# A bilinear form on one core: weight loads regrouped into fourteen GpSimd transfers, and y spread by VectorE transposes

## The chip, the cores and the metric

The kernel runs on one core of a Trainium2 chip. The metric is device time in microseconds (us) for one execution. The time before is the median of four runs; the profile is of one more execution.

## What is computed

```python
def setup_inputs():
    batch, dim_i, dim_j, dim_k = 32, 256, 256, 128
    ...

def reference(x, y, weight):
    return np.einsum('bi,bj,kij->bk', x, y, weight).astype(np.float32)
```

x is (batch, dim_i), y (batch, dim_j) and weight (dim_k, dim_i, dim_j), all float32. For each of 128 values of k there is a 256 x 256 matrix. The output for a batch row b and a k is x[b] times that matrix times y[b]. The weights are 33.55 MB in float32; x, y and the output are 32, 32 and 16 KB.

## The kernel before, in words

**Groups.** The 128 values of k are cut into 32 groups of four: group g holds k = g, g + 32, g + 64 and g + 96 (KK = 4 values, G = 32 groups). A group is 1 MiB in float32. Its 128 partitions are (ip, kk): 32 blocks of i by the four k, and in each partition lie 8 rows i (IC = 8) of 256 j, 8 KiB that are contiguous in DRAM. `w_v` (L47) is this view; in it the four k of a group are 8 MiB apart.

**Loads.** Group 0 is loaded as float32 by SyncE (L82) into `w0` and turned into bfloat16 by ScalarE (L112). All other groups are loaded by GpSimd's queue, which converts float32 to bfloat16 on the way into `w_sb` (L94 to L101): one transfer each for groups 1 to 30, and four for the last group, in pieces of 4, 2, 1 and 1 of the 8 rows (`LAST`). Each transfer has its own semaphore. After the second one GpSimd makes the identity matrix `ident` (L103, L104). GpSimd issues in this order and waits for nothing but its own memset; no buffer is reused, so no load waits for compute.

**Left operand.** VectorE builds `xblk` (L126 to L153): x is repeated four times (`x_rep`), put on the partitions by four 32-wide transposes (L132), and multiplied by a mask taken from `ident` (L142), once for each kk (L147). For each of the 8 rows ic this gives a 128 x 128 bfloat16 matrix that multiplies the four k of a group at once, with the result on 128 partitions (b, kk).

**y.** `y4` is y on the same 128 partitions (b, kk). VectorE makes a 32 x 128 `spread` matrix from the identity (L139), TensorE (PE) multiplies y by it in float32 (L157), and VectorE copies the result out of PSUM (L162).

**Units.** The groups are worked on in units of 8, 8, 6, 4, 3, 2 and 1 (`UNITS`). In a unit the groups go in pairs, one PSUM bank for each pair. For each ic in turn PE runs one matmul for each pair (128 x 512, or 128 x 256 for a single group; L166, recorded by the helper `product`), and the eight ic add up in PSUM. The first matmul of a pair waits for the semaphores of its two groups (L197); for the last group each piece is waited for at its first ic (L195). So the first matmul of a pair can run when its own groups are there, and everything after the last pair's first matmul waits for the whole unit. Then VectorE multiplies the unit's sums by `y4` (L216, PSUM to SBUF) and adds up over j (L220) into the unit's columns of `acc`; for the unit of one both are one instruction (L224). Units take PSUM banks in turn; PE waits before a unit until VectorE has read the banks it takes (L186).

**End.** SyncE stores `acc` (L233) when VectorE is done.

The order on each engine is the order of these statements; there is no scheduler that changes it. The order of loading is that of the loop at L94, and DMA transfers of one queue are worked through in the order of their issue.

Of the kernel before, what the change touches and what calls it, by code (L numbers as in the profile page):

```python
# [6 lines left out]


UNITS = (8, 8, 6, 4, 3, 2, 1)

LAST = ((0, 4), (4, 6), (6, 7), (7, 8))
BANKS = 8
# [3 lines left out]
def kernel(  # L16
# [24 lines left out]
    assert sum(UNITS) == G and UNITS[-1] == 1 and B == 32  # L41

    def sbuf(name, shape, dtype):
        return nc.alloc_sbuf_tensor(name, shape, dtype).ap()


    w_v = weight.rearrange("(kk g) (ip ic) j -> g ip kk (ic j)", kk=KK, ic=IC)  # L47

    w_sb = sbuf("w_sb", [P, G, IC * J], bf16)
    w0 = sbuf("w0", [P, IC * J], f32)  # L50
    x_sb = sbuf("x_sb", [B, I], f32)
    y_sb = sbuf("y_sb", [B, J], f32)
    ident = sbuf("ident", [P, P], f32)
    mask = sbuf("mask", [P, KK], f32)
    spread = sbuf("spread", [B, B, KK], f32)
# [4 lines left out]
    tmp = sbuf("tmp", [P, 2, max(UNITS), J], f32)  # L60
    acc = sbuf("acc", [P, G], f32)
    ps = nc.alloc_psum_tensor("ps", [P, BANKS, 2, J], f32).ap()


    s_w = [nc.alloc_semaphore(f"w{g}") for g in range(1, G - 1)]
# [13 lines left out]


    for ins in (
        nc.sync.dma_start(out=w0, in_=w_v[0]).then_inc(s_w0, 16),  # L82
        nc.scalar.dma_start(out=x_sb, in_=x).then_inc(s_x, 16),
        nc.scalar.dma_start(out=y_sb, in_=y).then_inc(s_y, 16),
    ):
        tc.no_tile_sem_insts.add(ins.ins.name)
# [4 lines left out]
    pool, act, v, pe, sp = nc.gpsimd, nc.scalar, nc.vector, nc.tensor, nc.sync  # L91


    for g in range(1, G):  # L94
        if g < G - 1:
            pool.dma_start(out=w_sb[:, g, :], in_=w_v[g]).then_inc(s_w[g - 1], 16)  # L96
# [12 lines left out]

    for h in range(2):  # L110
        lo, hi = h * IC * J // 2, (h + 1) * IC * J // 2
        c = act.copy(out=w_sb[:, 0, lo:hi], in_=w0[:, lo:hi])  # L112
        if h == 0:
            c._wait_ge(s_w0, 16)
        c.then_inc(s_act, 1)
# [4 lines left out]
    def done(ins):  # L120
        nonlocal n_dve
        n_dve += 1
        ins.then_inc(s_dve, 1)
        return n_dve

    t = done(v.tensor_copy(  # L126
        out=x_rep,
        in_=x_sb.rearrange("b (ip ic) -> b ic ip", ic=IC).unsqueeze(3)
        .to_broadcast([B, IC, IP, KK]),
    )._wait_ge(s_x, 16))  # L130
    for q in range(Q):
# [10 lines left out]
    t = done(v.tensor_reduce(  # L142
        out=mask, in_=ident.rearrange("p (ip kk) -> p kk ip", kk=KK), axis=AX, op=add,
    ))

    for kk in range(KK):
        c = v.tensor_scalar(  # L147
            out=xblk[:, :, :, kk], in0=xt, scalar1=mask[:, kk:kk + 1],
            scalar2=None, op0=mult,
        )  # L150
# [2 lines left out]
        t_x = done(c)  # L153


    pe.wait_ge(s_y, 16)
    pe.matmul(  # L157
        out=ps[:, BANKS - 1, 0, :], lhsT=spread.rearrange("p b kk -> p (b kk)"),
        rhs=y_sb, start=True, stop=True,
    )._wait_ge(s_dve, t_spread).then_inc(s_pe, 1)  # L160
    n_pe = 1
    t_y = done(v.tensor_copy(out=y4, in_=ps[:, BANKS - 1, 0, :])._wait_ge(s_pe, n_pe))  # L162
    v.wait_ge(s_dve, t_y)

    def product(out, lhsT, rhs, first, last, load):
        return pe.add_instruction(mybir.InstMatmult(  # L166
            name=nc.get_next_instruction_name(), engine=mybir.EngineType.PE,
            ins=[pe.lower_ap(rhs), pe.lower_ap(lhsT)], outs=[pe.lower_ap(out)],
            start_tensor_calc=first, stop_tensor_calc=last,
            tile_size=(P, P), tile_position=(0, 0), ldweights=load,  # L170
        ))

    pe.wait_ge(s_dve, t_x)
    at_dve = t_x
    freed = [0] * (BANKS - 1) + [t_y]
    g0 = bank = 0
    held = None
    for u, n_g in enumerate(UNITS):

        n_b = (n_g + 1) // 2  # L180
        if bank + n_b > BANKS:
            bank = 0
        pairs = [(bank + h, g0 + 2 * h, min(2, n_g - 2 * h)) for h in range(n_b)]
        free = max(freed[bank:bank + n_b])
        if free > at_dve:
            pe.wait_ge(s_dve, free)  # L186
            at_dve = free

        up = (len(UNITS) - 1 - u) % 2 == 0
        order = range(IC) if up else range(IC - 1, -1, -1)  # L190
        for n_ic, ic in enumerate(order):
            for b, g, n in pairs:
                waits = []
                if g == G - 1:
                    waits = [s for s, (lo, _) in zip(s_last, LAST) if lo == ic]  # L195
                elif n_ic == 0:
                    waits = [s_w[h - 1] for h in range(max(g, 1), g + n)]  # L197
                if n_ic == 0 and g == 0:
                    pe.wait_ge(s_act, 2)
                for s in waits[:-1]:  # L200
                    pe.wait_ge(s, 16)
                c = product(
                    ps[:, b, :n, :], xblk[:, ic, :, :].rearrange("p b kk -> p (b kk)"),
                    w_sb[:, g:g + n, ic * J:(ic + 1) * J],
                    first=(n_ic == 0), last=(n_ic == IC - 1), load=(held != ic),
                )
                held = ic
                if waits:
                    c._wait_ge(waits[-1], 16)
                if n_ic == IC - 1 and g + n == g0 + n_g:  # L210
                    c.then_inc(s_pe, 1)
        n_pe += 1
        prod = tmp[:, u % 2, :n_g, :]
        sums = ps[:, bank:bank + n_b, :, :].rearrange("p a h j -> p (a h) j")[:, :n_g, :]
        if n_g > 1:
            t = done(v.tensor_tensor(  # L216
                out=prod, in0=sums, in1=y4.unsqueeze(1).to_broadcast([P, n_g, J]), op=mult,
            )._wait_ge(s_pe, n_pe))
            freed[bank:bank + n_b] = [t] * n_b
            done(v.tensor_reduce(  # L220
                out=acc[:, g0:g0 + n_g], in_=prod, axis=AX, op=add,
            )._wait_ge(s_dve, t))
        else:
            done(v.tensor_tensor_reduce(  # L224
                out=prod[:, 0, :], in0=sums[:, 0, :], in1=y4, scale=1.0, scalar=0.0,
                op0=mult, op1=add, accum_out=acc[:, g0:g0 + 1],
            )._wait_ge(s_pe, n_pe))
        bank += n_b
        g0 += n_g


    out_v = out.rearrange("b (kk g) -> b kk g", kk=KK)
# [37 lines left out]
```

## Time and profile before

| | before |
|---|---|
| median of four runs | 86.81 us (86.5 to 87.32) |
| profiled execution, its own time | 86.88 us |
| its span, first to last instruction | 85.4 us |
| PE busy | 40.5 us (47%), 138 matmuls |
| VectorE (DVE) busy | 23.3 us (27%) |
| GpSimd (POOL) busy | 19.9 us (23%) |
| GpSimd queue: packets, bytes written | 4896, 16.26 MB |
| HBM read | 33.62 MB, 394 GB/s over the span |
| mean granted PE clock | 0.86 |

The profile's own execution took 86.88 us, of which 85.4 are the span from the first to the last instruction; 1.5 us lie around it. The page divides the span into 40 slices and gives each engine's busy share in tenths; "PEclk" is the clock that PE was granted and "GB/s" what DMA moved, counted at the writing side. The chain of work is followed back from the last instruction to what released it. "DVE" is VectorE, "POOL" GpSimd, "SP" SyncE, "PEld" PE's weight loads. Line numbers (L166) are those of the kernel before.

### The profile page before, as it was taken

The page shows a single profiled execution, that of the slowest core. Times are in us where ns is not written, and L with a number is a line of the kernel's source. Part 1 is how long each engine was busy: PE and PEld are TensorE (multiplying, and loading weights), DVE is VectorE, ACT ScalarE, POOL GpSimd, SP SyncE. Part 2 cuts the span into 40 slices and gives each one's busy share as a digit, 9 for nine tenths or more (in the row PEclk, how much of TensorE's full clock was granted, in tenths as well). Part 3 has the DMA queues.
Part 4 walks back from the last instruction along what each step waited for, and adds up shares of the span by engine and source line. Part 5 has one row for each costly group of instructions (what it writes and reads, how often), then busy time and mean ns, then how long its engine had stood idle before and what let it go on. Part 6 is the DMA issues. An engine that isn't in the chain of part 4 may idle for free.

```text
span 85.4 us, 323 instructions
## 1 busy us (share of the span) xinstructions
PE 40.5 (47%) x138; PEld 6.2 (7%) x52; DVE 23.3 (27%) x26; ACT 3.3 (4%) x3; POOL 19.9 (23%) x40
## 2 busy tenths in 40 slices
PE   0052002020199961020099992009997392099980
PEld 0020000000000100000010100001110020022240
DVE  0893000000000049700000009910003937300672
ACT  0635000000000000000000000000000000000000
POOL 0699999999600000000000000000000000000000
PEclk9999999999999999955556999975569999755699
DMA  0999999999999999999999999999999999999930
GB/s 15 365 282 213 213 213 200 211 213 211 211 215 215 215 213 213 211 211 207 213 213 215 215 215 211 215 215 213 213 215 215 215 213 213 213 211 208 198 51 8
DMA packets 5280, 17.39 MB, mean 204 GB/s; under 512 B 736, under 2 KB 1184, under 8 KB 5152
## 3 DMA queue, kind: packets, MB, share of 16 engines
q0 software_dynamic: 4896, 16.26, 95.9%
q1 hardware_dynamic: 288, 1.07, 3.3%
q10 hardware_dynamic: 96, 0.07, 0.3%
HBM read 33.62 MB, written 0.02 MB: 394 GB/s over the span
## 4 chain that ended last, share of the span: by engine, by line
DMA 50%; PE 22%; POOL 14%; another core or an unknown queue 6%; DVE 2%; issue 1%; POOLq 0%
DMA w_sb<-in_weight_dram 50%; PE ps L166 22%; POOL w_sb L96 13%; DVE tmp L216 1%; DVE acc L220 1%; DVE tmp L224 0%; POOL ident L104 0%; POOL ident L103 0%; POOLq L89 0%; DVE acc L224 0%
## 5 line engine op out<-in xcount | busy, mean ns | idle before, releaser
L166 PE MATMUL ps<-w_sb,xblk 128*128 128x512 bf16 (+1 forms) x136 | 39.3, 450 | 37.1 <-DMA w_sb<-in_weight_dram 37.0
L216 DVE TENSOR_TENSOR tmp<-ps,y 128x2048 f32<-128x2048 f32 (+4 forms) x6 | 9.2, 1536 | 57.8 <-PE ps L166 57.8
L96 POOL DMA_DIRECT2D w_sb<-in_weight_dram x30 | 17.1, 773 | 2.4 <-POOLq L89 2.4
L166 PEld LDWEIGHTS ps<-w_sb,xblk 128*128 128x128 bf16 x50 | 5.7, 113 | 71.2 <-issue 68.4
L220 DVE TENSOR_REDUCE acc<-tmp 128x8 f32<-128x2048 f32 (+4 forms) x6 | 9.2, 1530 | 0.2
L157 PE MATMUL ps<-y_sb,spread 32*128 32x256 f32 x2 | 1.2, 710 | 5.3 <-DVE spread L139 5.3
L99 POOL DMA_DIRECT2D w_sb<-in_weight_dram x4 | 2.6, 1057 | 0.0
L112 ACT CAST w_sb<-w 128x1024 bf16<-128x1024 f32 x2 | 2.0, 1043 | 2.0 <-DMA w<-in_weight_dram 2.0
L132 DVE STREAM_TRANSPOSE xt<-x_rep 32x256 f32<-32x256 f32 x4 | 1.7, 435 | 0.1
L147 DVE TENSOR_SCALAR xblk<-xt,mask 128x256 bf16<-128x256 f32 x4 | 1.4, 499 | 0.0
L112 ACT ACT_TABLE_LOAD x1 | 1.3, 1283 | 2.4 <-PEq L89 2.4
L126 DVE COPY x_rep<-x_sb 32x1024 f32<-32x1024 f32 x1 | 0.7, 681 | 2.4 <-PEq L89 2.4
L157 PEld LDWEIGHTS ps<-y_sb,spread 32*128 32x128 f32 x2 | 0.5, 308 | 5.3 <-DVE spread L139 5.3
L162 DVE COPY y<-ps 128x256 f32<-128x256 f32 x1 | 0.4, 436 | 0.0
L224 DVE CUSTOM_DVE_ANT_0 tmp<-ps,y 128x256 f32<-128x256 f32 x1 | 0.4, 414 | 0.0
L142 DVE TENSOR_REDUCE mask<-ident 128x4 f32<-128x128 f32 x1 | 0.4, 357 | 0.0
L104 POOL TENSOR_SCALAR_AFFINE_SELECT ident<-ident 128x128 f32<-128x128 f32 x1 | 0.3, 287 | 0.1
L103 POOL MEMSET ident<- 128x128 f32 x1 | 0.2, 248 | 0.0
L139 DVE COPY spread<-ident 32x128 f32<-32x128 f32 x1 | 0.2, 215 | 0.0
L254 POOL MEMSET const-float32-0.0<- 128x1 f32 x1 | 0.1, 99 | 0.2 <-issue 0.2
L254 POOL MEMSET const-bfloat16-1.0<- 128x1 bf16 x1 | 0.1, 102 | 0.0
L254 POOL MEMSET const-uint8-127<- 128x1 uint8 x1 | 0.1, 102 | 0.0
(2 smaller groups left out, 0.2 us busy)
## 6 DMA issues: line engine op xcount, KB each, us to landing
w_sb<-in_weight_dram POOLq DMA_DIRECT2D x30, 512.0 KB, 32.1
w<-in_weight_dram SPq DMA_DIRECT2D x1, 1024.0 KB, 4.9
w_sb<-in_weight_dram POOLq DMA_DIRECT2D x1, 256.0 KB, 61.0
w_sb<-in_weight_dram POOLq DMA_DIRECT2D x1, 128.0 KB, 61.1
w_sb<-in_weight_dram POOLq DMA_DIRECT2D x2, 64.0 KB, 60.9
x_sb<-in_x_dram ACTq DMA_DIRECT2D x1, 32.0 KB, 1.6
y_sb<-in_y_dram ACTq DMA_DIRECT2D x1, 32.0 KB, 3.6
out_dram<-acc SPq DMA_DIRECT2D x1, 16.0 KB, 1.4
```

The costliest lines, as they stand in the source:

```text
L96: pool.dma_start(out=w_sb[:, g, :], in_=w_v[g]).then_inc(s_w[g - 1], 16)
L99: pool.dma_start(out=w_sb[:, g, lo * J:hi * J], in_=w_v[g][:, :, lo * J:hi * J],).then_inc(s, 16)
L112: c = act.copy(out=w_sb[:, 0, lo:hi], in_=w0[:, lo:hi])
L126: t = done(v.tensor_copy(out=x_rep, in_=x_sb.rearrange("b (ip ic) -> b ic ip", ic=IC).unsqueeze(3) .to_broadcast([B, IC, IP, KK]),)._wait_ ...
L132: c = v.transpose(out=xt[q * 32:(q + 1) * 32, :, :], in_=x_rep[:, :, q * IP // Q:(q + 1) * IP // Q, :],)
L142: t = done(v.tensor_reduce(out=mask, in_=ident.rearrange("p (ip kk) -> p kk ip", kk=KK), axis=AX, op=add,))
L147: c = v.tensor_scalar(out=xblk[:, :, :, kk], in0=xt, scalar1=mask[:, kk:kk + 1], scalar2=None, op0=mult,)
L157: pe.matmul(out=ps[:, BANKS - 1, 0, :], lhsT=spread.rearrange("p b kk -> p (b kk)"), rhs=y_sb, start=True, stop=True,)._wait_ge(s_dve, t_s ...
L162: t_y = done(v.tensor_copy(out=y4, in_=ps[:, BANKS - 1, 0, :])._wait_ge(s_pe, n_pe))
L166: return pe.add_instruction(mybir.InstMatmult(name=nc.get_next_instruction_name(), engine=mybir.EngineType.PE, ins=[pe.lower_ap(rhs), pe.l ...
L216: t = done(v.tensor_tensor(out=prod, in0=sums, in1=y4.unsqueeze(1).to_broadcast([P, n_g, J]), op=mult,)._wait_ge(s_pe, n_pe))
L220: done(v.tensor_reduce(out=acc[:, g0:g0 + n_g], in_=prod, axis=AX, op=add,)._wait_ge(s_dve, t))
```

## The change

The groups stay the same sets of four k, but loads, units and the places in `w_sb` are rearranged.

- `LOADS` lists ten GpSimd transfers of 1, 2, 4, 8, 4, 2, 4, 2, 1 and 2 groups; after them come the four pieces of the last group, which is now group 23. With group 0, which SyncE still loads, this covers all 32 groups. A transfer has one semaphore, whatever its size.
- The groups of one transfer are equally spaced (every 4th, 8th, 16th), so that the values of k in it are equally spaced too: a transfer of n groups reads, for each ip, 4n rows at one step (1 MiB for eight groups, 2 MiB for four, 4 MiB for two, 8 MiB for one). In each partition it writes n stretches of 4 KiB, at places in `w_sb` that are equally spaced as well.
- `UNITS` still has 8, 8, 6, 4, 3, 2 and 1 groups, named by number. `place_of` gives the place of a group in `w_sb`, so that a unit's groups lie side by side. The first matmul of a pair waits for the transfers that its groups are in, if no earlier matmul has waited for them: unit 0 waits for the first three transfers, unit 1 for that of eight, the unit of six for those of four and two, the unit of four for one of four, the unit of three for those of two and one, the unit of two for one of two, the last for the four pieces.
- VectorE's reduce writes columns of `acc` that are equally spaced; where the groups of a unit are not, there are two reduces: 4 + 2 for the unit of six, 2 + 1 for the unit of three.
- GpSimd makes `ident` after its second transfer, as before, which now is the one of groups 8 and 24.
- `y4` is made without PE: VectorE transposes y in blocks of 32 (`yt`), repeats it four times along kk (`y_rep`), and transposes the result onto the partitions in four instructions. `spread`, the two-pass float32 matmul and the copy from PSUM go.

PE's number of product matmuls and their shapes and order do not change.

```diff
-UNITS = (8, 8, 6, 4, 3, 2, 1)
+UNITS = (
+    tuple(range(0, 32, 4)),
+    tuple(range(1, 32, 4)),
+    (2, 10, 18, 26, 6, 22),
+    (3, 11, 19, 27),
+    (14, 30, 7),
+    (15, 31),
+    (23,),
+)
+LOADS = (
+    (16,), (8, 24), (4, 12, 20, 28), tuple(range(1, 32, 4)), (2, 10, 18, 26),
+    (6, 22), (3, 11, 19, 27), (14, 30), (7,), (15, 31),
+)
...
-    w_v = weight.rearrange("(kk g) (ip ic) j -> g ip kk (ic j)", kk=KK, ic=IC)
+    def rows_of(groups):
+        step = G // len(groups)
+        assert all(g == groups[0] + n * step for n, g in enumerate(groups))
+        v = weight.rearrange("(u s) (ip ic) j -> s ip u (ic j)", s=step, ic=IC)
+        return v[groups[0]]
+
+    def w_of(groups):
+        at = [place_of[g] for g in groups]
+        step = at[1] - at[0] if len(at) > 1 else 1
+        assert all(a == at[0] + n * step for n, a in enumerate(at))
+        return w_sb[:, at[0]:at[-1] + 1:step, :]
...
-    for g in range(1, G):
-        if g < G - 1:
-            pool.dma_start(out=w_sb[:, g, :], in_=w_v[g]).then_inc(s_w[g - 1], 16)
-        else:
-            for s, (lo, hi) in zip(s_last, LAST):
-                pool.dma_start(
-                    out=w_sb[:, g, lo * J:hi * J], in_=w_v[g][:, :, lo * J:hi * J],
-                ).then_inc(s, 16)
-        if g == 2:
+    for n, (load, s) in enumerate(zip(LOADS, s_w)):
+        pool.dma_start(out=w_of(load), in_=rows_of(load)).then_inc(s, 16)
+        if n == 1:
             pool.memset(ident, 0.0).then_inc(s_pool, 1)
...
+    for s, (lo, hi) in zip(s_last, LAST):
+        pool.dma_start(
+            out=w_sb[:, G - 1, lo * J:hi * J],
+            in_=rows_of(UNITS[-1])[:, :, lo * J:hi * J],
+        ).then_inc(s, 16)
...
-    t_spread = done(v.tensor_copy(
-        out=spread, in_=ident[:B, :B].unsqueeze(2).to_broadcast([B, B, KK]),
-    )._wait_ge(s_pool, 2))
...
-    pe.matmul(
-        out=ps[:, BANKS - 1, 0, :], lhsT=spread.rearrange("p b kk -> p (b kk)"),
-        rhs=y_sb, start=True, stop=True,
-    )._wait_ge(s_dve, t_spread).then_inc(s_pe, 1)
-    n_pe = 1
-    t_y = done(v.tensor_copy(out=y4, in_=ps[:, BANKS - 1, 0, :])._wait_ge(s_pe, n_pe))
-    v.wait_ge(s_dve, t_y)
+    t = done(v.transpose(
+        out=yt, in_=y_sb.rearrange("b (jb j) -> b jb j", j=32),
+    )._wait_ge(s_y, 16))
+    t = done(v.tensor_copy(
+        out=y_rep, in_=yt.unsqueeze(3).to_broadcast([B, J // 32, B, KK]),
+    )._wait_ge(s_dve, t))
+    BQ = B // Q
+    for q in range(Q):
+        c = v.transpose(
+            out=y4[q * 32:(q + 1) * 32, :].rearrange("p (jb j) -> p jb j", j=32),
+            in_=y_rep[:, :, q * BQ:(q + 1) * BQ, :],
+        )
...
+                need = [sem_of[g] for g in places[at:at + n] if g in sem_of]
+                need = [s for n_s, s in enumerate(need)
+                        if s.num not in landed and s not in need[:n_s]]
+                if u == len(UNITS) - 1:
+                    need = [s for s, (lo, _) in zip(s_last, LAST) if lo == ic]
+                landed |= {s.num for s in need}
...
-            done(v.tensor_reduce(
-                out=acc[:, g0:g0 + n_g], in_=prod, axis=AX, op=add,
-            )._wait_ge(s_dve, t))
+            lo = 0
+            while lo < n_g:
+                hi = lo + 1
+                while hi < n_g and unit[hi] - unit[hi - 1] == unit[lo + 1] - unit[lo]:
+                    hi += 1
+                step = unit[lo + 1] - unit[lo] if hi - lo > 1 else 1
+                c = v.tensor_reduce(
+                    out=acc[:, unit[lo]:unit[hi - 1] + 1:step], in_=prod[:, lo:hi, :],
+                    axis=AX, op=add,
+                )
...
```

More of the change, by code (lines that the diff above doesn't have):

```diff
@@ L40 @@
     assert KK * B == P and IP * KK == P and IC * IP == I and G * KK == K
-    assert sum(UNITS) == G and UNITS[-1] == 1 and B == 32
+    places = [g for unit in UNITS for g in unit]
+    place_of = {g: i for i, g in enumerate(places)}
+    assert sorted(places) == list(range(G)) and len(UNITS[-1]) == 1 and B == 32
     def sbuf(name, shape, dtype):
         return nc.alloc_sbuf_tensor(name, shape, dtype).ap()
-    w_v = weight.rearrange("(kk g) (ip ic) j -> g ip kk (ic j)", kk=KK, ic=IC)
+    def rows_of(groups):
[8 more added lines that the diff above has]
+        return w_sb[:, at[0]:at[-1] + 1:step, :]
     w_sb = sbuf("w_sb", [P, G, IC * J], bf16)
@@ L54 @@
     mask = sbuf("mask", [P, KK], f32)
-    spread = sbuf("spread", [B, B, KK], f32)
+    yt = sbuf("yt", [B, J // 32, B], f32)
+    y_rep = sbuf("y_rep", [B, J // 32, B, KK], f32)
     x_rep = sbuf("x_rep", [B, IC, IP, KK], f32)
@@ L59 @@
     y4 = sbuf("y4", [P, J], f32)
-    tmp = sbuf("tmp", [P, 2, max(UNITS), J], f32)
+    tmp = sbuf("tmp", [P, 2, max(map(len, UNITS)), J], f32)
     acc = sbuf("acc", [P, G], f32)
     ps = nc.alloc_psum_tensor("ps", [P, BANKS, 2, J], f32).ap()
-    s_w = [nc.alloc_semaphore(f"w{g}") for g in range(1, G - 1)]
+    s_w = [nc.alloc_semaphore(f"w{load[0]}") for load in LOADS]
+    sem_of = {g: s for s, load in zip(s_w, LOADS) for g in load}
     s_last = [nc.alloc_semaphore(f"wl{lo}") for lo, _ in LAST]
@@ L81 @@
     for ins in (
-        nc.sync.dma_start(out=w0, in_=w_v[0]).then_inc(s_w0, 16),
+        nc.sync.dma_start(out=w0, in_=rows_of((0,))).then_inc(s_w0, 16),
         nc.scalar.dma_start(out=x_sb, in_=x).then_inc(s_x, 16),
@@ L107 @@
             )._wait_ge(s_pool, 1).then_inc(s_pool, 1)
+    for s, (lo, hi) in zip(s_last, LAST):
[3 more added lines that the diff above has]
+        ).then_inc(s, 16)
     for h in range(2):
         lo, hi = h * IC * J // 2, (h + 1) * IC * J // 2
-        c = act.copy(out=w_sb[:, 0, lo:hi], in_=w0[:, lo:hi])
+        c = act.copy(out=w_sb[:, place_of[0], lo:hi], in_=w0[:, lo:hi])
         if h == 0:
@@ L138 @@
         done(c)
-    t_spread = done(v.tensor_copy(
-        out=spread, in_=ident[:B, :B].unsqueeze(2).to_broadcast([B, B, KK]),
-    )._wait_ge(s_pool, 2))
     t = done(v.tensor_reduce(
         out=mask, in_=ident.rearrange("p (ip kk) -> p kk ip", kk=KK), axis=AX, op=add,
-    ))
+    )._wait_ge(s_pool, 2))
     for kk in range(KK):
@@ L153 @@
         t_x = done(c)
-    pe.wait_ge(s_y, 16)
-    pe.matmul(
-        out=ps[:, BANKS - 1, 0, :], lhsT=spread.rearrange("p b kk -> p (b kk)"),
-        rhs=y_sb, start=True, stop=True,
-    )._wait_ge(s_dve, t_spread).then_inc(s_pe, 1)
-    n_pe = 1
-    t_y = done(v.tensor_copy(out=y4, in_=ps[:, BANKS - 1, 0, :])._wait_ge(s_pe, n_pe))
-    v.wait_ge(s_dve, t_y)
+    t = done(v.transpose(
[10 more added lines that the diff above has]
+        )
+        if q == 0:
+            c._wait_ge(s_dve, t)
+        t = done(c)
+    v.wait_ge(s_dve, t)
     def product(out, lhsT, rhs, first, last, load):
@@ L171, in product @@
         ))
+    pe.wait_ge(s_act, 2)
     pe.wait_ge(s_dve, t_x)
     at_dve = t_x
-    freed = [0] * (BANKS - 1) + [t_y]
-    g0 = bank = 0
+    n_pe = 0
+    freed = [0] * BANKS
+    landed = set()
+    p0 = bank = 0
     held = None
-    for u, n_g in enumerate(UNITS):
+    for u, unit in enumerate(UNITS):
+        n_g = len(unit)
         n_b = (n_g + 1) // 2
@@ L182 @@
             bank = 0
-        pairs = [(bank + h, g0 + 2 * h, min(2, n_g - 2 * h)) for h in range(n_b)]
         free = max(freed[bank:bank + n_b])
@@ L191 @@
         for n_ic, ic in enumerate(order):
[L192 to L200, printed above, removed]
+            for h in range(n_b):
+                n = min(2, n_g - 2 * h)
+                at = p0 + 2 * h
+                need = [sem_of[g] for g in places[at:at + n] if g in sem_of]
[4 more added lines that the diff above has]
+                landed |= {s.num for s in need}
+                for s in need[:-1]:
                     pe.wait_ge(s, 16)
                 c = product(
-                    ps[:, b, :n, :], xblk[:, ic, :, :].rearrange("p b kk -> p (b kk)"),
-                    w_sb[:, g:g + n, ic * J:(ic + 1) * J],
+                    ps[:, bank + h, :n, :],
+                    xblk[:, ic, :, :].rearrange("p b kk -> p (b kk)"),
+                    w_sb[:, at:at + n, ic * J:(ic + 1) * J],
                     first=(n_ic == 0), last=(n_ic == IC - 1), load=(held != ic),
@@ L207 @@
                 held = ic
-                if waits:
-                    c._wait_ge(waits[-1], 16)
-                if n_ic == IC - 1 and g + n == g0 + n_g:
+                if need:
+                    c._wait_ge(need[-1], 16)
+                if n_ic == IC - 1 and h == n_b - 1:
                     c.then_inc(s_pe, 1)
@@ L219 @@
             freed[bank:bank + n_b] = [t] * n_b
-            done(v.tensor_reduce(
-                out=acc[:, g0:g0 + n_g], in_=prod, axis=AX, op=add,
-            )._wait_ge(s_dve, t))
+            lo = 0
[8 more added lines that the diff above has]
+                )
+                if lo == 0:
+                    c._wait_ge(s_dve, t)
+                done(c)
+                lo = hi
         else:
@@ L225 @@
                 out=prod[:, 0, :], in0=sums[:, 0, :], in1=y4, scale=1.0, scalar=0.0,
-                op0=mult, op1=add, accum_out=acc[:, g0:g0 + 1],
+                op0=mult, op1=add, accum_out=acc[:, unit[0]:unit[0] + 1],
             )._wait_ge(s_pe, n_pe))
         bank += n_b
-        g0 += n_g
+        p0 += n_g
     out_v = out.rearrange("b (kk g) -> b kk g", kk=KK)
```

## The prediction

> **What bounds the kernel now.** I read the page's slices first, then the queue table, then the chain of work that ended last, then VectorE's timeline at the end, and last the duration spread of the GpSimd transfers.
>
> The slices (40 of 2.13 us each) and the queue table of the page:
>
> ```profile
> span 85.4 us, 323 instructions
> ...
> PE   0052002020199961020099992009997392099980
> ...
> DVE  0893000000000049700000009910003937300672
> ...
> POOL 0699999999600000000000000000000000000000
> PEclk9999999999999999955556999975569999755699
> DMA  0999999999999999999999999999999999999930
> GB/s 15 365 282 213 213 213 200 211 213 211 211 215 215 215 213 213 211 211 207 213 213 215 215 215 211 215 215 213 213 215 215 215 213 213 213 211 208 198 51 8
> ...
> q0 software_dynamic: 4896, 16.26, 95.9%
> ```
>
> DMA is full from slice 2 to slice 38; no compute engine is. GpSimd has issued everything by slice 11 and the queue then works on for 60 us, so the rate of the 16 DMA engines sets the landings, not the issue. 213 GB/s is what is written (bf16); the reads are f32, twice that, about 426 GB/s. The 4896 packets of q0 are 34 transfers of 128 data packets plus 16 semaphore packets, one of these on each engine: 34 x 144 = 4896.
>
> The chain that ended last, in order of time:
>
> ```profile
> 14.81 42.78 DMA w_sb<-in_weight_dram
> ...
> 74.84 4.85 PE ps L166 x15
> 79.69 0.06 another core or an unknown queue
> 79.75 0.04 issue
> 79.80 2.29 PE ps L166 x8
> 82.08 0.02 issue
> 82.11 0.70 DVE tmp L216
> 82.81 0.02 issue
> 82.83 0.69 DVE acc L220
> 83.52 0.33 DVE tmp L224
> ```
>
> 42.78 us of it is one block of DMA. At the end it goes through the unit of two groups: its second group lands at 79.74 us, PE multiplies it in 2.29 us, VectorE multiplies and reduces it (0.70 + 0.69), and the last group's fused step (0.33) waits for VectorE, not for its own data. So the end is the landing of the last but one group plus about 4.1 us, and PE had ended the unit before only 0.1 us ahead of that landing. VectorE's timeline there gives the slack:
>
> ```profile
> 79.73 0.96 DVE L216 TENSOR_TENSOR tmp<-ps,y 128x768 f32<-128x768 f32 x1 [6.35 <-PE ps L166]
> 80.72 0.95 DVE L220 TENSOR_REDUCE acc<-tmp 128x3 f32<-128x768 f32 x1
> 82.11 0.69 DVE L216 TENSOR_TENSOR tmp<-ps,y 128x512 f32<-128x512 f32 x1 [0.43 <-PE ps L166]
> ```
>
> VectorE is idle 0.43 us between the unit of three and the unit of two.
>
> And the spread of the issues on GpSimd, minimum/median/maximum ns:
>
> ```profile
> L96 POOL DMA_DIRECT2D w_sb<-in_weight_dram x30: 552/752/1355, 2.9 to 19.5; - x30
> ```
>
> Their starts are 0.518 us apart; one of 1355 ns, begun at 5.69 us, is the exception.
>
> **The change, part by part.**
>
> *Fewer transfers (34 to 14).* The bytes are the same: 30 whole groups and four pieces, 128 data packets each. What goes is 20 semaphore packets on every engine. In the trace's packet records a data packet (8192 bytes read, 4096 written) starts 304.5 ns after the one before it on its engine, and a semaphore packet takes 22 ns between two of them: 8 x 304.5 + 22 = 2458 ns for a group, which is the pace of landings I find (2.457 us; L166's waits end 2.46 us apart at 72.38 and 74.84). On the path: 20 x 22 ns = **0.44 us less**. The rule that speaks for much more is in the Trainium skill, "DMA: Bandwidth & Descriptors", section "Anatomy of one DMA": each GpSimd transfer costs about 2.0 us fixed plus its bytes at 436 GB/s. Paid one after another that would give 20 x 2.0 = 40 us. The trace disagrees: 2.458 us for 1 MiB is 427 GB/s, with no room for a fixed part, since transfers overlap in the queue. I take 0.44.
>
> *The early slip.* The first ten or so landings are not 2.457 but up to 2.52 us apart, 0.27 us too much in sum, and data packets over 330 ns (324 is normal) occur only up to 27 us, while GpSimd writes descriptors (until 22.6 us) and shortly after. If the writing disturbs the packets, what counts is how long it goes on in the changed kernel: between 14 x 0.52 = 7 us if an issue costs per instruction, and 31 x 0.52 + 3 x 0.52 = 18 us if it costs per 128 packets. The same row fits both, since every transfer has 128 data packets now. So between 0 and 0.2 us less; I take 0.1, nearer to the per-packet end, where nothing is gained.
>
> *Do the longer issues arrive in time?* The first transfer stays one group; its first packet moves at 4.83 us, 1.3 us after its issue ends. Priced per packet (0.52 us a group), the second (2 groups) is written by 4.6 and needed at 7.7 us, when the first has drained; then memset and affine_select (0.56 us), then 2.1 us for four groups, by about 7.3, needed at 12.6; then 4.2 us for eight, by 11.5, needed at 22.4. With 1.3 us to the first packet each has 2 us or more to spare: cost nothing.
>
> *A rule against this.* The 1355 ns issue stalls 0.8 us while VectorE runs the four L147 TENSOR_SCALAR (5.55 to 6.92 us). The Trainium skill, "SBUF — State Buffer", the box on the trap "DVE blocks DMA" (section on the two sides of SBUF), says why: a VectorE copy or scalar operation between SBUF operands can hold the port through which GpSimd writes descriptors, and the DMA engines starve. The change adds such a copy (y_rep, 32x1024 f32; 681 ns by the equal x_rep row L126) just there. By the rule the third transfer comes up to 0.8 + 0.7 = 1.5 us later, packets at about 10.1 us instead of 8.6. By the trace, DMA stayed full through the stall of before because of queued work; here 4.9 us of groups 8 and 24 last until 12.6. Cost nothing, with 2.5 us of cover; without cover it would be 1.5 us.
>
> *y by transposes.* Removed: the spread copy (215 ns), two PE passes (1.2 us), the PSUM copy (436 ns). Added on VectorE: five transposes at 435 ns (row L132) and the copy at 681 ns, 2.9 us. y4 is then ready at about 10 us instead of 7.2; its first reader, L216, starts at 31.0. PE's wait for xblk moves with mask: ident comes after three groups of issues instead of two, 0.5 us, so xblk is at about 7.4; PE needs all of unit 0's eight groups, at 22 us. Hidden by 20 us of loading.
>
> *PE and waits by transfer.* Unit 0 waits for the third transfer, unit 1 for the one of eight, the unit of four for one of four. PE already ran only the first matmul of a pair before its unit was complete (single matmuls at 33.06, 37.97), so at most three matmuls, 0.4 to 1.3 us, move behind a landing, and PE idles before the next unit (66 to 67, 71 to 72). The unit of three still waits for 2 then 1, the unit of two for 2 as before, the last group for its four pieces. VectorE's reduces split 6 = 4 + 2 and 3 = 2 + 1: from rows of 1752, 1219 and 686 ns, +0.15 us each. The first is hidden by idle time; the second lies in the 0.43 us slack at 81.68. Without that slack 0.15 us; I take 0.
>
> *Sum.* 0.44 + 0.1 = 0.54 off the span: 85.4 to 84.85, and the profiled execution 86.88 to 86.35. That execution is 0.07 above the median 86.81, so the median goes to about **86.3 us**, 0.6% less.
>
> **The rivals.**
>
> *B, the packets themselves run closer.* For: long runs of descriptors reach the engines in one piece, and the slip could go entirely. Against: 304.5 ns is steady for 60 us whatever lies between. The page named first gives a fabric ceiling of 435 GB/s, 301.2 ns a packet: 248 packets x 3.3 ns = 0.8 us as an outer end. With 0.44 and 0.27: 85.3 us.
>
> *C, the gain does not reach the end.* PE's clock was at half from 73.8 to 80.6 us. Granted late, it makes the eight matmuls of the unit of two 8 x 0.427 = 3.4 us instead of about 1.9, and the reduce's slack may be gone. 0.5 us eats the gain: 86.8. The runs shown scatter from 86.5 to 87.3, as such a phase would.
>
> *D, slower: the new order of reads.* A transfer of eight reads, for each partition, eight rows 1 MiB apart, before it goes to the next; now there are four rows 8 MiB apart. If HBM serves that worse, every packet of 30 groups pays. It cancels the gain at 0.44/240 = 1.8 ns a packet (0.6%); at 2%, 6.1 ns, 240 x 6.1 = 1.5 us longer, 87.8. Against: at each moment the 16 engines still read neighbouring 8 KiB rows, and 8 MiB steps run at 427 GB/s.
>
> *E, descriptors late.* GpSimd needs over 0.95 us a group (0.52 measured) before the third transfer misses 12.6 us; at 1.2 us it starves for 6 x 0.25 = 1.5 us: 87.8. The nested pattern could cost that, but twice the row is far.
>
> **How the numbers follow.** The forecast 0.5 (own range 85.8 to 86.8), B 0.2, C 0.1, D 0.12, E 0.08. A measurement of this kernel can tell about 1% (0.87 us) from no change. Faster by more: most of B and the low edge of the forecast, 0.24. Slower by more: most of D and E, 0.18. The rest, 0.58. The range leaves out the far half of B and of D and E: 85.4 to 87.6.
>
> **What would show it.** Right: q0 has 31 x 128 + 3 x 128 + 14 x 16 = 4576 packets; DMA is full from slice 2; the unit of two lands 0.4 to 0.6 us earlier, at about 79.2; two-group landings are 4.89 us apart. B: data packets below 304 ns apart. D: above 306, GB/s under 211. E: a slice before 25 us with DMA below 9. C: landings earlier, but a tail after the landing of the unit of two above 4.2 us. The forecast is wrong if the packet pace moves by over 1% or the queue runs dry once.

## The result, and the profile after

| | before | after |
|---|---|---|
| median of all executions | 86.87 us (86.11 to 88.31, 58) | 86.86 us (85.7 to 88.76, 39) |
| their lower and upper quartile | 86.58, 87.32 us | 86.06, 87.66 us |
| ratio | 1 | **0.9947**, 95% interval 0.9923 to 0.9972 |
| profiled execution, its span | 86.88, 85.4 us | 87.24, 85.9 us |
| GpSimd queue: packets | 4896 | 4576 |
| GpSimd's last issue ends | 22.6 us | 13.6 us |
| unit of two: second group landed | 79.75 us | 79.29 us |
| store of the output issued | 83.88 us | 83.03 us |

By the ratio the change is a gain of 0.5%, 0.46 us. The ratio counts, of each kernel, only the executions within 1.5% of its own fastest (24 of 39 after, by this rule 45 of 58 before); with one limit for both, 87.4 us, the means are 86.76 and 86.38 us, a ratio of 0.9956.

Over all executions the gain is not seen: the medians are equal, the lower quartile falls by 0.52 us and the upper one rises by 0.34. A part of the reason is on record. A time is longer than the span by 1.3 to 1.6 us as a rule. With the changed kernel it is longer by over 1.8 us in 10 of these 39 executions, and in 18 of the 63 of its three series (these, e1 and f2 below); with the kernel before in 1 of the 81 that were run beside the experiments. The median span of the same 63 and 81 executions is 85.1 and 85.6 us. So the span becomes shorter by about 0.5 us, and in a good quarter of the executions more than that is lost around it. Why was not tried; the last section has the one profile that bears on it.

In the profiled execution of the changed kernel the store of the output took longer than before, so the end is also read from a second profile of the same kernel (e1 below).

The slices and queues of the page after, of 2.15 us each:

```profile
span 85.9 us, 292 instructions
...
PE   0000000000299990000199996039990781396920
...
DVE  0899400000000009910000006940009609004660
...
POOL 0699993000000000000000000000000000000000
PEclk9999999999999999975555899755699999956998
DMA  0999999999999999999999999999999999999900
GB/s 19 355 278 200 215 214 214 215 214 215 212 215 214 215 215 215 217 215 215 214 215 215 214 217 212 215 214 214 214 215 214 215 215 214 214 214 205 161 8 8
...
q0 software_dynamic: 4576, 16.25, 94.6%
...
q8 instruction: 1, 0.02, 0.1%
```

q0 has 320 packets fewer, 20 on each of 16 engines. DMA is as full as before and moves 214 to 215 GB/s, before 211 to 215. PE starts only in slice 11 (23 us), when the eight groups of unit 0 are there, and POOL stops at slice 7 instead of 11. The last line is new: one packet of instructions, of which more below.

The chain that ended last, from the landing of the unit of three on:

```profile
74.39 4.09 PE ps L199 x15
78.49 0.80 another core or an unknown queue
79.29 0.04 issue
79.33 1.90 PE ps L199 x8
81.23 0.02 issue
81.26 0.70 DVE tmp L254
81.96 0.02 issue
81.98 0.69 DVE acc L265
82.67 0.33 DVE tmp L274
```

It is the same chain. PE now waits 0.80 us for the landing (the line about an unknown queue is that wait); before it waited 0.06. The store's issue, before and then after:

```profile
83.88 0.35 SPq L233 DMA_DIRECT2D out_dram<-acc  x1
```

```profile
83.03 0.34 SPq L283 DMA_DIRECT2D out_dram<-acc  x1
```

From the landing of the unit of two to the store's issue it is 3.74 us; before 4.13, since PE took 2.29 us for these eight matmuls, begun at half clock.

What SyncE's queue waited for, in this execution and then in the second profile:

```profile
SPq L289 <- DMA out_dram<-acc: 2.5, 1, 2.5
```

```profile
SPq L289 <- DMA out_dram<-acc: 1.1, 1, 1.1
```

The store took 2.9 us to land instead of 1.4. In the packet records the one packet of q8, 16 KB of instructions, lasts from 83.36 to 84.81 us. Fifteen of the store's sixteen parts had landed by 84.46; the packets of the sixteenth begin at 84.80, as that packet ends. Without it this span would have been about 84.5.

GpSimd's whole-group transfers after the change, and before it:

```profile
L124 POOL DMA_DIRECT2D w_sb<-in_weight_dram x10: 568/703/1737, 2.9 to 10.8; - x10
...
DMA to landing us min/median/max: 5.4/47.1/68.5
```

```profile
DMA to landing us min/median/max: 5.2/32.1/60.3
```

An issue takes 568 ns for one group, about 700 for two, 762 to 802 for four. The eight-group one is the 1737. The first transfer, of one group in both kernels, landed 5.4 us after its issue instead of 5.2: its first packet moved at 5.12 us instead of 4.84.

### The profile page after: what moved, and what is told of

It is laid out like the page before. It is cut to its first block, busy times and chain, and to the rows that moved or that the text cites. A ratio compares the mean times of both kernels' runs of the same rounds, so it can differ in the third digit from the quotient of the medians.

```text
span 85.9 us, 292 instructions
## 1 busy us (share of the span) xinstructions
PE 37.4 (44%) x136; PEld 5.5 (6%) x50; DVE 25.7 (30%) x32; ACT 3.3 (4%) x3; POOL 10.9 (13%) x20
## 3 DMA queue, kind: packets, MB, share of 16 engines
q0 software_dynamic: 4576, 16.25, 94.6%
## 4 chain that ended last, share of the span: by engine, by line
DMA 57%; PE 20%; another core or an unknown queue 8%; POOL 6%; DVE 2%; issue 1%; POOLq 0%
DMA w_sb<-in_weight_dram 57%; PE ps L199 20%; POOL w_sb L124 5%; DVE tmp L254 1%; DVE acc L265 1%; DVE tmp L274 0%; POOL ident L127 0%; POOL ident L126 0%; POOLq L118 0%; DVE acc L274 0%
## 5 line engine op out<-in xcount | busy, mean ns | idle before, releaser
L199 PE MATMUL ps<-w_sb,xblk 128*128 128x512 bf16 (+1 forms) x136 | 37.4, 441 | 44.8 <-DMA w_sb<-in_weight_dram 44.7
L265 DVE TENSOR_REDUCE acc<-tmp 128x2 f32<-128x512 f32 (+3 forms) x8 | 9.3, 1185 | 0.2
L124 POOL DMA_DIRECT2D w_sb<-in_weight_dram x10 | 8.0, 810 | 2.4 <-POOLq L118 2.4
L132 POOL DMA_DIRECT2D w_sb<-in_weight_dram x4 | 2.2, 556 | 0.0
L189 DVE STREAM_TRANSPOSE y<-y_rep 32x256 f32<-32x256 f32 x4 | 1.7, 435 | 0.1
L184 DVE COPY y_rep<-yt 32x1024 f32<-32x1024 f32 x1 | 0.7, 693 | 0.0
```

Source lines behind the costliest of these rows:

```text
L124: pool.dma_start(out=w_of(load), in_=rows_of(load)).then_inc(s, 16)
L132: pool.dma_start(out=w_sb[:, G - 1, lo * J:hi * J], in_=rows_of(UNITS[-1])[:, :, lo * J:hi * J],).then_inc(s, 16)
L184: t = done(v.tensor_copy(out=y_rep, in_=yt.unsqueeze(3).to_broadcast([B, J // 32, B, KK]),)._wait_ge(s_dve, t))
L189: c = v.transpose(out=y4[q * 32:(q + 1) * 32, :].rearrange("p (jb j) -> p jb j", j=32), in_=y_rep[:, :, q * BQ:(q + 1) * BQ, :],)
L199: return pe.add_instruction(mybir.InstMatmult(name=nc.get_next_instruction_name(), engine=mybir.EngineType.PE, ins=[pe.lower_ap(rhs), pe.l ...
L265: c = v.tensor_reduce(out=acc[:, unit[lo]:unit[hi - 1] + 1:step], in_=prod[:, lo:hi, :], axis=AX, op=add,)
```

## The experiments

Four things vary from one execution to the next: when the first group has landed, what PE's clock is at the end, whether a packet of instructions comes in between, and how much time lies around the span. So each run is read in two ways, by its ratio and by a stretch that these hardly touch: from the landing of the first whole group of GpSimd's queue to that of the unit of two (20 semaphore packets on each engine apart). From the records of packets and semaphores in the profiles:

| transfers | first group landed to unit of two landed, us | mean |
|---|---|---|
| 34 | before 71.69, e2 71.27, e3 71.40, f4 71.33 | 71.42 |
| 14 | after 70.98, e1 70.91, e4 70.87, e5 70.86, e6 70.98, e7 70.98, f2 70.86, f3 71.02 | 70.93 |

(e8 and f1 are told in their places.) The stretch leaves out the first load. From the first packet of GpSimd's queue, the landing of the unit of two comes after 74.81 us with 34 transfers (74.76 to 74.92) and after 74.42 with 14 (74.18 to 74.73). That is 0.39 us instead of 0.49, since the first group took 0.1 us longer on the mean with 14; these ranges do not meet either, but nearly.

**e1, the changed kernel again** (no edit).

> The changed kernel once more, for a second profile whose end is not disturbed. Theory (20 semaphore packets of 22 ns fewer on each engine, and GpSimd done with its descriptors earlier): from the first packet of the GpSimd queue to the last landing about 76.8 us against 77.5 before, the unit of two landing 0.4 to 0.7 us earlier, span about 84.5, ratio to before 0.992 to 0.998. Rival (the first profile's gain was an accident of its start): landings within 0.2 us of those of before.

Ratio 0.9955 (0.9919 to 0.9992), span of the profile 84.6 us. First packet to last landing 76.94 us. The unit of two landed at 79.40, 0.35 us earlier than before (expected 0.4 to 0.7), though the first group landed 0.4 us later (8.49 against 8.06). The gain in landings is no accident of the first profile. The span is 0.75 us shorter than before; 0.35 of it is the landing, and most of the rest PE's clock, full here at the end (3.75 us to the store's issue against 4.13).

**e2, singles.** The changed kernel with one transfer for each group.

```diff
-LOADS = (
-    (16,), (8, 24), (4, 12, 20, 28), tuple(range(1, 32, 4)), (2, 10, 18, 26),
-    (6, 22), (3, 11, 19, 27), (14, 30), (7,), (15, 31),
-)
+LOADS = tuple((g,) for unit in UNITS for g in unit if g not in (0, 23))
```

> The changed kernel with each group as a transfer of its own again (34 transfers), in the changed order, with the changed places, units and y. Theory: the whole gain comes from the number of transfers, so this is as slow as before: ratio 0.998 to 1.002, 2.457 us from landing to landing, GpSimd issuing until about 22 us and 0.2 to 0.3 us of slip in the first ten landings. Rival (the order of groups, the units' waits or the y path give the gain): ratio near 0.995 as for the changed kernel, landings as there.

Ratio 1.0004 (0.9953 to 1.0055): no gain is left, with the order of groups, the units and the y path as changed, though the interval reaches into that of e1. The landings decide: the stretch is that of 34 transfers. First packet to last landing 77.42 us. GpSimd issues until 23.0 us. One part of the expectation failed: its landings are 2.457 us apart almost from the start, without the slip.

**e3, y alone.** The kernel before, with `y4` made by the VectorE lines of the change (the `-`/`+` lines of `spread`, the matmul, `yt` and `y_rep` in the diff above) and nothing else.

> The kernel before with y spread by VectorE transposes, nothing else changed. Theory: y4 is ready at about 10 us and first read at 31, so nothing moves: ratio 0.998 to 1.002. Rival (the two float32 passes of PE, or the copy that holds GpSimd up, count): ratio outside that, with a landing of the unit of two that is moved by over 0.2 us.

Ratio 1.004 (0.9987 to 1.0093), no gain, and above the expected range; the landing stretch is that of 34 transfers. It may be a loss: the median of all twelve executions is 88.02 us against 86.92 for the kernel before beside it (35), and that of the spans 86.6 against 85.6. The landings do not explain it: that of the unit of two came at 79.85 us, 0.1 later than before. In this profile a packet of instructions lay on the store, which took 2.9 us. Why most executions of this run are longer was not tried.

**e4, merge alone.** The changed kernel with `y4` made by PE as before (the same lines, put back).

> The changed kernel with y spread by PE as before; loads, places, units and waits as changed. Theory: all of the gain is here: ratio 0.992 to 0.997, landings as in the changed kernel. Rival (the y path is part of the gain): ratio between 0.997 and 1.

Ratio 0.9992 (0.9949 to 1.0035). The stretch of landings, 70.87 us, is that of the changed kernel, but the ratio is above the expected range, lies in the rival's, and its interval holds both 1 and 0.995. Nine executions count in it. Their spans are 85.02 us on the mean, against 85.37 for the kernel before beside them; but two of them, of 87.2 us with spans of 84.9, have 2.3 us around the span. So the span shows the gain and the time does not.

The profile, of an execution of 87.91 us that the ratio does not count, shows another thing that blurs the times. Two stretches (granted clock is the third column from the right) and then PE, VectorE and the store in the timeline:

```profile
77.40:79.70 2.30, 0.02 (x1) 0.00 (x0) 1.97 (x3) 0.00 (x0) 0.00 (x0) 1.00 1.06 207
79.70:83.20 3.50, 3.43 (x9) 1.07 (x8) 0.00 (x0) 0.00 (x0) 0.00 (x0) 0.51 0.63 95
```

```profile
79.77 4.42 PE L193 MATMUL ps<-w_sb,xblk 128*128 128x512 bf16 x16 [2.35 <-DMA w_sb<-in_weight_dram]
83.36 0.69 DVE L247 TENSOR_TENSOR tmp<-ps,y 128x512 f32<-128x512 f32 x1 [3.90 <-PE ps L193]
...
85.14 0.34 SPq L276 DMA_DIRECT2D out_dram<-acc  x1
```

PE had finished the unit of three early and idled 2.35 us; at 79.74, as the unit of two landed, the clock went to half, for 3.41 us. The unit took 3.59 us to reach VectorE instead of 1.9, and the store was issued 5.41 us after the landing instead of 3.74. That is 1.67 us, over three times the gain.

**e5, fused.** The changed kernel with the last unit's fused step in the units of three and two as well.

```diff
-        if n_g > 1:
+        if n_g > 3:
...
-            done(v.tensor_tensor_reduce(
-                out=prod[:, 0, :], in0=sums[:, 0, :], in1=y4, scale=1.0, scalar=0.0,
-                op0=mult, op1=add, accum_out=acc[:, unit[0]:unit[0] + 1],
-            )._wait_ge(s_pe, n_pe))
+            for n, g in enumerate(unit):
+                c = v.tensor_tensor_reduce(
+                    out=one[:, p0 + n - (G - 6), :], in0=sums[:, n, :], in1=y4, scale=1.0, scalar=0.0,
+                    op0=mult, op1=add, accum_out=acc[:, g:g + 1],
+                )
+                if n == 0:
+                    c._wait_ge(s_pe, n_pe)
+                t = done(c)
+            freed[bank:bank + n_b] = [t] * n_b
```

> The changed kernel, with VectorE's fused multiply and sum, one instruction of about 0.41 us for a group, in the units of three and two as in the last one. Theory (the end is a chain from the landing of the unit of two through PE and VectorE): the two steps of 0.70 and 0.69 us become two of some 0.4, so the store is issued about 0.4 us earlier after that landing, 3.3 to 3.4 us instead of 3.74 with PE at full clock; ratio to before 0.988 to 0.993. Rival (the end hangs on the last group's landing alone): no change against the changed kernel, 0.995.

Ratio 0.9821 (0.9723 to 0.992), below the expected range, from two of six executions; the profile itself met a half clock at 79.59 us. It was run again as f3.

**e6, warm.** The changed kernel with extra matmuls in PE's gaps, into a PSUM bank that no one reads before the unit of two overwrites it.

```diff
+    def keep(n):
+        for _ in range(n):
+            product(
+                ps[:, BANKS - 1, :, :],
+                xblk[:, held, :, :].rearrange("p b kk -> p (b kk)"),
+                w_sb[:, 0:2, 0:J], first=True, last=True, load=False,
+            )
...
+                if keeping:
+                    keep(8)
+        if u in (2, 3, 4):
...
+            keep({2: 8, 3: 6, 4: 7}[u])
```

> The changed kernel with 29 extra 128x512 matmuls, whose results nobody reads, in PE's gaps before the units of four, three and two. Theory (PE's clock at half is what lengthens the end in some executions, because PE idles in the window before): the granted clock is full from about 64 us on, the unit of two takes 1.9 us and the store is issued 3.7 us after its landing; the fastest runs stay, the median comes nearer to them; ratio 0.990 to 0.995. Rival (the clock does not follow PE's idle time, or the extra matmuls delay real ones): tails of over 4.1 us after the landing remain, ratio 0.995 or more.

Ratio 0.9894 (0.9837 to 0.995), at the low edge of the expected range. The same two stretches:

```profile
77.00:79.20 2.20, 1.40 (x7) 0.00 (x0) 1.89 (x3) 0.00 (x0) 0.00 (x0) 1.00 1.05 206
79.20:82.00 2.80, 2.72 (x16) 1.36 (x14) 0.76 (x2) 0.00 (x0) 0.00 (x0) 1.00 0.90 140
```

PE is busy 1.40 of 2.20 us in the gap and its clock stays full (from 60.0 us to the end of the span); the store is issued 3.74 us after the landing. Over the whole span the six executions had a mean granted clock of 0.90 to 0.92, the kernel before beside them 0.84 to 0.88. The clock follows PE's idle time.

**e7, both.** e5 and e6 together.

> Both of these: fused steps and extra matmuls. Theory: the two add up, the store 3.3 to 3.4 us after the landing of the unit of two, ratio 0.985 to 0.991. Rival: no better than the better of the two alone.

Ratio 0.9849 (0.9792 to 0.9906). The intervals of e5, e6 and e7 overlap, so the ratios do not tell whether the two add up. VectorE at its end:

```profile
81.52 0.42 DVE L295 CUSTOM_DVE_ANT_0 one<-ps,y 128x256 f32<-128x256 f32 x1 [3.11 <-PE ps L200]
...
81.87 0.42 DVE L295 CUSTOM_DVE_ANT_0 one<-ps,y 128x256 f32<-128x256 f32 x1
...
82.56 0.42 DVE L295 CUSTOM_DVE_ANT_0 one<-ps,y 128x256 f32<-128x256 f32 x1 [0.27 <-PE ps L200]
```

The unit of two takes VectorE 0.7 us instead of 1.4, and the last step now waits 0.27 us for PE and the last landing. The store is issued 3.47 us after the landing of the unit of two, 0.27 less than in e6; the expected 3.3 to 3.4 was too low because of that new wait.

**e8, both, with singles.** e7 with the `LOADS` of e2.

> The same with each group as a transfer of its own: 34 transfers instead of 14 behind an end that PE's clock does not move. Theory (20 semaphore packets of 22 ns): 0.44 to 0.6 us slower than with 14 transfers, and from the first packet of the GpSimd queue to the last landing 77.3 to 77.5 us against 76.8 to 77.0. Rival (the number of transfers counts for nothing, the gain was chance in the end): within 0.15 us of it.

A miss: ratio 0.9832 (0.9779 to 0.9886), not slower than e7, from six executions each, with mean spans of 85.00 and 84.97 us. Its profile cannot be used for the landings as it stands. The chain:

```profile
75.09 4.05 PE ps L198 x22
79.14 1.66 another core or an unknown queue
80.80 0.04 issue
```

The unit of two was due 2.45 us after the group before it (77.50) and came after 3.30: the one packet of instructions, 945 ns from 78.46 us, falls into that time. The stretch of landings is 72.32 us; less 0.85 it is 71.47, that of 34 transfers. The time of this pair stayed open, and f3 and f4 were made for it.

**f1, small transfers.** The changed kernel with 40 more transfers of almost nothing.

```diff
+        if n >= 5:
+            for m in range(8 * (n - 5), 8 * (n - 4)):
+                pool.dma_start(
+                    out=small[:, 2 * m:2 * m + 2], in_=x[0:16, 2 * m:2 * m + 2],
+                ).then_inc(s_small, 16)
...
+    sp.wait_ge(s_small, 16 * 40)
```

> The changed kernel with 40 more GpSimd transfers between its own, each of 8 bytes into 16 partitions: on every engine one packet of 8 bytes and one semaphore packet, 40 x 32 packets in all; nobody reads what they bring. Theory (a transfer costs its semaphore packet, 22 ns, and its data packets, on every engine): from the first packet of the GpSimd queue to the last landing at least 40 x 22 = 0.9 us more than 76.9, and 1.8 to 2.2 us more if a packet of 8 bytes takes as long as a semaphore packet or a little longer; time longer by the same. Rival (the fixed part of a transfer is hidden by the others in the queue): under 0.3 us more.

Ratio 1.0043 (1.0007 to 1.0079). Its queue:

```profile
q0 software_dynamic: 5856, 16.26, 93.8%
```

That is 1280 packets more. First packet to last landing took 77.89 us, against 77.03 on the mean of the eight with 14 transfers: 0.86 us. But 0.31 of it lies ahead of the small transfers, in the first group, which landed 3.80 us after the first packet instead of 3.49. In the stretch of landings, which holds 32 of the 40, it is 71.41 against 70.93, 0.48 us, or 15 ns for each. A small packet behind a small packet takes 9 ns, not 22; 22 ns is what a semaphore packet takes between data packets. So the small transfers cost some 0.55 us: more than the rival (hidden) allows, less than the theory's 0.9, which holds with a lower price where small packets follow one another.

**f2, the changed kernel a third time** (no edit).

> The changed kernel a third time, as the neighbour of the other three on the same chip. Theory: ratio to before 0.992 to 0.998, its fastest executions with a span of 84.4 to 84.7.

Ratio 1.0011 (0.9967 to 1.0055), outside the expected range, though the fastest executions have spans of 84.7 and 85.0 us, and the stretch of landings is 70.86. In the profile the first group landed only at 8.96 us, 0.9 later than in the profile of before, and the clock was at half until 80.7, so that the store came 4.15 us after the landing. The spans of the eight executions in the ratio are 85.28 us on the mean, those of the kernel before beside them 85.38. A gain of 0.5 us can vanish in a dozen executions.

**f3, fused again** (the edit of e5).

> The changed kernel with VectorE's fused step in the units of three and two, a second time, for a profile in which PE's clock is full at the end. Theory: the store issued 3.3 to 3.4 us after the landing of the unit of two; fastest executions with a span 0.3 to 0.4 us under those of the changed kernel; ratio to before 0.987 to 0.994. Rival: no difference against the changed kernel.

Ratio 0.9893 (0.9866 to 0.992). The fastest spans are 84.1 and 84.2 us, 0.3 us under those of the first series and 0.6 under those of f2. Its profile met the half clock again (unit of two to store 4.95 us), so the expected 3.3 to 3.4 was not seen in it; e7's 3.47 is the number for a full clock. The ratio lies under that of f2, the changed kernel on the same chip, and the intervals do not touch.

**f4, fused with singles** (the edits of e5 and e2).

> The same with 34 transfers instead of 14, without extra matmuls. Theory (20 semaphore packets): fastest executions 0.4 to 0.6 us slower than those of its twin with 14 transfers, and 77.3 to 77.5 us from the first packet of the GpSimd queue to the last landing. Rival (as in the pair with extra matmuls, no difference shows in the time): within 0.15 us.

Ratio 0.9973 (0.9934 to 1.0011), against 0.9893 (0.9866 to 0.992) for its twin with 14 transfers on the same chip: the intervals do not touch. Fastest spans 84.7 against 84.1 us, landings as of 34. Mean spans of the executions in the ratio, 34 transfers against 14: 85.12 and 84.41 here, 85.70 and 84.83 for e2 and e1, 85.00 and 84.97 for e8 and e7. So two of three pairs show the merging in the time, by more (0.7 and 0.9 us) than the 0.4 to 0.5 us of the landings, and one does not show it. Of the time, only the direction is supported; the size rests on the landings.

## Why the prediction was right, point by point

The theory was: 20 semaphore packets fewer on every engine, 22 ns each, on a queue that is never empty. Its rivals among the causes were the order and waits of the units, the y path, and chance.

- *The 0.44 us.* Landings come 71.42 - 70.93 = 0.49 us sooner, in eight profiles against four, with ranges that do not meet (70.86 to 71.02, 71.27 to 71.69). Within one transfer the price shows by itself: the eight groups of unit 1 land in 19.52 us as one transfer (e1) and in 19.66 as eight (e2), 0.14 us for seven semaphore packets, 20 ns each. Undoing the merging alone undoes the gain in the landings (e2; f4 against f3); doing y alone brings none (e3). Shown for the landings; in the time it is clear in two pairs of three. The 2.0 us fixed cost of the section "Anatomy of one DMA" in the Trainium skill, "DMA: Bandwidth & Descriptors", does not come off here: landings 2.457 us apart for 1 MiB leave no room for it.
- *The early slip, 0.1 us.* Not shown. The first landing-to-landing time of before is 2.59 us, not 2.52 at most, and the slip sums to 0.4 us, not 0.27. The other three profiles with 34 transfers in the table exceed 29 x 2.457 = 71.25 us by 0.15 or less; without the profile of before the difference is 0.40 us, which the semaphore packets cover. e2, with GpSimd writing until 23.0 us, has no slip, so the length of GpSimd's writing does not decide it. What does stayed open, and that 0.44 + 0.1 comes near the 0.49 is luck in the 0.1.
- *The price of an issue.* I took the per-packet end (0.52 us a group). Measured: 0.57 us for one group, 0.70 for two, 0.76 to 0.80 for four; an issue costs mostly per instruction. It has no weight here, since the queue never ran dry, and rival E is out.
- *VectorE against GpSimd's descriptors.* The stall came, where the four xblk operations are: the eight-group issue, begun at 5.53 us, took 1737 ns. In e4 the stall fell on the next issue and the eight-group one took 884, so it is some 0.85 us (0.80 before). The new copy `y_rep`, begun at 7.06 us, met the end of that issue and then a four-group issue of 802 ns, against 762 and 767 for the others: 0.04 us. That does not refute the rule on the trap "DVE blocks DMA" (the Trainium skill, "SBUF — State Buffer"): in e2, e3, e8 and f4 the same copy began 0.16 us after the issue of a single group, and this took 965 to 977 ns, where the kernel before took 552 at the same place. So a copy of 0.68 us can cost an issue 0.42, and next to none where the issue starts behind it. Neither cost time here.
- *Order of reads.* 214 to 215 GB/s; a transfer of eight lands in 19.52 us, 64 packets at 304.7 ns each with its semaphore packet. Rivals B and D are out.
- *Tail.* The second reduce of the unit of three was hidden (0.73 us of idle VectorE remained), as said. The forecast left the 4.13 us behind the landing as they were. In the profile after and in e1 they are 3.74 and 3.75, because PE's clock happened to be full: another 0.4 us off these spans, by luck. Rival C was undersized: it gave 0.5 us to a late clock, though its own sum, 3.4 less 1.9, is 1.5; e4 shows 1.67.

The forecast of 0.6% stands against 0.5% (0.3 to 0.8) in the ratio. Its median of 86.3 us was not reached over all executions (86.86): neither the packet of instructions nor the longer time around the span is in the forecast.

## What to carry to other kernels

Here, where the DMA queue stayed full, merging transfers took off their semaphore packets, about 20 ns each, and no fixed part. Where a trace shows such a queue, count the packets on each engine and take their spacing from the trace; the estimate of the gain is the number of semaphore packets saved times their spacing. A gain of half a microsecond is then easier to prove between two landings than in the total time, where the clock, the end and the time around the span vary by more. And when the loads set the pace, look at the chain behind the last landings: with VectorE's fused step there as well as the merged transfers the ratio to before is 0.9893 (f3).

## What the runs showed of the hardware that was not expected

- PE's granted clock is full or half, and the stretches of half clock that lie whole in these profiles last 3.41 us or a multiple of it, at a phase that differs between executions. In e4 the clock went to half at 79.74 us for 3.41 us; in the 3.41 us before, PE was idle for 2.3. In e1 PE idled as long in one piece (77.05 to 79.40) with no effect. Counted in steps of 3.41 us from the end of its last half clock (70.64 us) a boundary falls at 77.47, inside the gap, and neither 3.41 us beside it has more than 2.0 us of idle time. So here a gap of 2.35 us was enough where it lay in one such stretch, and not where it lay across two. The gap in e1's chain:

```profile
74.51 2.54 PE ps L199 x15
77.05 2.35 another core or an unknown queue
79.40 0.04 issue
79.44 1.90 PE ps L199 x8
```

- One packet of 16 KB of instructions is fetched near the end in eight of the fourteen profiles (after, e1, e3, e5 to e8, f4); it takes 0.89 to 1.45 us. In the five where it falls on the store (after, e3, e5, e6, f4) the store takes 2.2 to 3.0 us to land, in the other nine 1.4. In e8 the landing of the unit of two came 0.85 us late with it. In e1 it ran from 85.83 to 86.96 us, after the end of the span (84.6); this execution's time, 86.72, is 2.1 us longer than its span, in the other thirteen 1.3 to 1.5. So it may be what lies around the span in the executions told with the result, but one profile does not show that. Which engine asks for it, and why it was not seen in the profiles of before, e2, e4, f1, f2 and f3, was not tried.
- The first whole group lands between 8.06 and 8.96 us in executions of the same first transfer (f1: 9.76). Single packets of group 0, on SyncE's queue, take 0.57 to 0.93 us there (f1: 1.66) instead of the usual 0.31; the cause was not sought.
